# Remainders of the MLP operands by accumulating DMAs, in place of GpSimd and part of VectorE

## The chip, the cores and the metric

The kernel runs on one core of a Trainium2 chip, as one program. The metric is the device time of one execution in microseconds (us). Three runs of the kernel before gave a median of 1139.48 us (1139.41 to 1142.07). Five engines work in parallel, each through its own instruction stream: TensorE (PE; its weight loads are shown apart as PEld), VectorE (DVE), ScalarE (ACT), GpSimd (POOL) and SyncE (SP, which here only issues DMAs).

## The reference

One layer of a hybrid decoder (sequence 1024, width 1024, all in float32): a mixer (S5 state space and windowed attention) and a gated MLP. Only the MLP is touched by the change:

```python
h2 = _rms(x, norm2_w[l]) * (1 + sc2) + sh2
x = x + g2 * _conv_ffn(h2, w_up[l], conv_w[l], conv_b[l], w_down[l])

def _conv_ffn(h, w_up, conv_w, conv_b, w_down):
    up = h @ w_up                      # 1024x1024 by 1024x5632
    up = causal depthwise conv of width 3 (up) + conv_b
    val, gate = jnp.split(up, 2, axis=-1)
    return (jax.nn.silu(gate) * val) @ w_down      # 1024x2816 by 2816x1024
```

## The kernel before

**Precision.** A float32 operand is held as two halves: hi, its rounding to the format fp32r that TensorE multiplies, and lo, the remainder, again in fp32r. `split` (L137 to 141) makes them from a 128x512 operand: ScalarE copies the operand to hi with the rounding (L133 in the trace, a CAST), then VectorE or GpSimd subtracts, lo = operand - hi (L118, a TENSOR_TENSOR). Every product is three matmuls of 128x512 (`mm3`, L143 to 147; they stand at L97 or L99 in the trace): hi by hi, hi by lo, lo by hi.

**Two products by Strassen-Winograd.** Both MLP products work on 2x2 blocks with 7 block products instead of 8, numbered i = 1 to 7. Products 1, 2 and 4 take a block of the weights as it lies in DRAM (1 and 2 from the first row of blocks, 4 the last block); 3, 5, 6 and 7 take sums of blocks, which VectorE makes in place on the loaded tiles.

**The up product.** 22 f-tiles (FFT), for each of them 7 products of 12 matmuls. `weight(f, i)` (L949 to 970) makes the weight halves: `raw` loads two 128x1024 tiles of w_up by SP (at first tW, later tX4, tX5, W0, W1), and `split` writes into a ring of ten slots (tU0 to tU5 and four quarters of tXQ), seven products ahead. In it the lo of i = 1, 2, 4 is GpSimd's, the rest VectorE's. `took` (L1037 to 1058) copies or adds the PSUM banks, `conv` and a Silu follow, and `gd[f]`, the gated product in DRAM, is stored by SP (L1197).

**The lead part.** For f = 0 to 3 the products 1 and 2 run early, while VectorE and ScalarE still prepare the normalized operands A[3] to A[7]. The order of the matmuls is pinned there until f = 1, i = 5. Behind the first of these products stands `rms(1)`, on which the normalized operands of the second half of the sequence wait.

**The down product.** The 11 block rows p (256 columns of the gated product each) go in three chunks of 3, 4 and 4. In each chunk the products come in the order 1, 5, 6, 3, 7, 2, 4, and in each of these all p of the chunk: 77 steps of 12 matmuls. `fetch` loads the four blocks of gd and of w_down of one p; `operands` (L1130 to 1148) makes the sums, and for the two operands of a step `mixed` (L1121 to 1126) takes the next of nine slots and calls `split`, with every third lo on GpSimd ("vvp"). Operands are made three steps ahead (AH). `put` adds four banks to the output on VectorE (L127) after each product of a chunk. In steps 24 to 27 and 33 to 36 VectorE also adds the residual (xo + xt).

A scheduler arranges the instructions of each engine by the estimated time line; data dependences are kept.

Of the kernel before, what the change touches and what calls it, by code (L numbers as in the profile page):

```python
# [14 lines left out]
ADD, SUB, MUL, MAX, MIN = ALU.add, ALU.subtract, ALU.mult, ALU.max, ALU.min  # L15
# [7 lines left out]
FFT = 22  # L23
# [39 lines left out]
def hymba_kernel(ctx, tc, xT, c, wmod, wu, wkvq, small, consts, relb, pq, wglu, wout, wup, wdn, out):  # L63
# [7 lines left out]
    def new(tag, dt=F32):  # L71
        return pool.tile([128, SIZES.get(tag, 1024)], dt, tag=tag, name="t" + tag)
# [11 lines left out]
    def newr(tag):  # L84
        return RT(new(tag, F32R))

    vec, act, pol, sync = nc.vector, nc.scalar, nc.gpsimd, nc.sync
# [29 lines left out]
    def tt(eng, o, a, b, op):  # L117
        return eng.tensor_tensor(out=o, in0=a, in1=b, op=op)  # L118
# [12 lines left out]
    def cpy(e, o, i):  # L131
        if e == "a":
            act.copy(o, i)  # L133
        else:
            ENG[e].tensor_copy(out=o, in_=i)

    def split(x, src, hi_eng="a", lo_eng="v"):  # L137

        hi, lo = x
        cpy(hi_eng, hi.r, src)  # L140
        tt(ENG[lo_eng], lo.r, src, hi.f, SUB)

    def mm3(o, a, b, start, stop, chain=False):  # L143

        pe.matmul(o, a[0].r, b[0].r, start=start, stop=False, skip_group_check=chain)
        pe.matmul(o, a[0].r, b[1].r, start=False, stop=False, skip_group_check=chain)
        pe.matmul(o, a[1].r, b[0].r, start=False, stop=stop, skip_group_check=chain)
# [7 lines left out]
    def half(t):  # L155
        return t[:, 0:512], t[:, 512:1024]
# [82 lines left out]
    for k in range(8):  # L239
        xk = xs[k % 4]  # L240
        sync.dma_start(out=xk, in_=xT[k])
        emit_mod(8 + k, early[:, (k % 3) * 1024:(k % 3 + 1) * 1024], cact)
        if k % 2 == 0:
            wst = new(("W0", "A10")[k // 2 % 2])
            sync.dma_start(out=wst, in_=wu[k // 2])
        w = half(newr(f"U{k}") if k < 4 else wux[:, (k - 4) * 1024:(k - 3) * 1024])
        wus.append(w)
        split(w, wst[:, (k % 2) * 512:(k % 2) * 512 + 512])
        stt(mods[:, k:k + 1], mod[:, 8 + k:9 + k], 1.0, n1s[:, k:k + 1], ADD, MUL)
        hi, lo = hT[k]  # L250
        act.activation(out=hi.r, in_=xk, func=AF.Identity, scale=mods[:, k:k + 1])
        stt(lo.r, xk, mods[:, k:k + 1], hi.f, MUL, SUB)
        sq = new(("A11", "A1")[k % 2])
        act.activation(out=sq, in_=xk, func=AF.Square)
        if k == 0:
            sync.dma_start(out=cn, in_=consts[:, 0:384])
        for h in range(2):
            pe.matmul(bank[6 + h], ones, sq[:, h * 512:h * 512 + 512], start=(k == 0), stop=(k == 7))
        if k == 1:
            Q12, P12, Bs_t = new("W1"), new("U5"), new("U4")  # L260
            sync.dma_start(out=Q12, in_=pq[0])
            sync.dma_start(out=P12, in_=pq[1])
        for j in range(6):
            mm3(bank[j], sl(hT[k], slice(j, 1024, T)), w, k == 0, k == 7)
# [194 lines left out]
    def head_w(t):  # L459
        wst = new("W0")  # L460
        sync.dma_start(out=wst, in_=wkvq[t])
        w = (newr(f"U{2 * (t % 2)}"), newr(f"U{2 * (t % 2) + 1}"))
        split(w, wst)
        if t >= 2:
            qn.append(new(("W1", "U4", "U5")[t - 2]) if t < 5 else qx)
        b, b2, r = abank(), abank(), brow[:, (t % 2) * 128:(t % 2 + 1) * 128]
        for k in range(8):
            ks = slice(k * 128, k * 128 + 128)
            pe.matmul(b[0:2, 0:128], shs[:, 2 * k:2 * k + 2], w[0].r[:, ks], start=(k == 0), stop=False)
            pe.matmul(b[0:2, 0:128], shs[:, 2 * k:2 * k + 2], w[1].r[:, ks], start=False, stop=(k == 7))  # L470
        vec.tensor_copy(out=r, in_=b[0:2, 0:128])
        with pe.pin(False):
            pe.matmul(b2[:, 0:1], r, ones[0:2, 0:1], start=True, stop=True)
        vec.tensor_copy(out=bcol[:, t:t + 1], in_=b2[:, 0:1])
        return w
# [145 lines left out]
    for q in range(4):  # L621
        sync.dma_start(out=kd[:, 8 * q:8 * q + 8, 112:240],
                       in_=ka[32 * q:32 * q + 16, :].rearrange("p (g x) -> p g x", x=128))
# [60 lines left out]
    for h in range(2):  # L684
        for i in range(4):
            q_ = newr(f"H{8 + 4 * h + i}")
            for kv in range(2):
# [3 lines left out]
                src = qn[i][p0, h * 512:h * 512 + 512]  # L691
# [51 lines left out]
    for h in range(2):  # L743
        for m in range(4):
            zs[m, h] = half(newr(f"A{m + 4 * h}"))
            split(zs[m, h], zT[m][:, h * 512:h * 512 + 512], pick("ZH", m))
# [16 lines left out]
    for h in range(2):  # L763
# [9 lines left out]
        for n in range(4):  # L773
            src = zT[n][:, hs]
# [6 lines left out]
        for n in range(4):  # L781
            src = zT[n][:, hs]
# [27 lines left out]
    for n in range(8):  # L810
        av = bank[2]
        for kv in range(2):
            u = 2 * n + kv
            w_ = 256 if n else 128
# [4 lines left out]
            for i2 in range(2):  # L819
# [6 lines left out]
                for i1 in range(2):  # L826
                    i = 2 * i2 + i1
                    vec.tensor_tensor_reduce(  # L828
                        out=P[:, i, :], in0=b[:, i1 * 256:i1 * 256 + w_], in1=Tb[kv][:, i, 256 - w_:256],
# [31 lines left out]
    x = [xq[:, k * 1024:(k + 1) * 1024] for k in range(4)] + [new(f"X{k}") for k in range(4, 8)]  # L861
# [33 lines left out]
    for i, d in enumerate(order):  # L895
        if i % 2 == 0:
# [3 lines left out]
            w = (t_[:, 0:1024], t_[:, 1024:2048])  # L900
# [41 lines left out]
    def raw(f, which):  # L942
        i = ri[0]
        ri[0] += 1
        t_ = new(raws[i] if i < LEADS else (("X4", "W0"), ("X5", "W1"))[which][f % 2])
        sync.dma_start(out=t_, in_=wup[f + FFT * which])
        wraw[f, which] = half(t_)

    def weight(f, i):  # L949
        i_ = wi_[0]  # L950
        tag = ptags[i_ if i_ < 2 * LEADS else 2 + (i_ - 2 * LEADS) % 10]
        wi_[0] += 1
        if not isinstance(tag, str) and not wq:
            wq.append(newr("XQ"))
        w = half(newr(tag) if isinstance(tag, str) else wq[0][:, tag * 1024:(tag + 1) * 1024])
        wp[f, i] = w
        if (f, 0) not in wraw:
            raw(f, 0)
        v1, v2 = wraw[f, 0]
        if i not in (1, 2) and (f, 1) not in wraw:  # L960
            raw(f, 1)
        g1, g2 = wraw.get((f, 1), (None, None))
        if i == 5:
            tt(vec, v1, v1, g1, SUB)
            tt(vec, g1, g1, g2, ADD)
        elif i == 6:
            tt(vec, g1, g2, v1, SUB)
        elif i == 3:
            tt(vec, g1, v2, g1, SUB)
        split(w, {1: v1, 2: v2, 3: g1, 4: g2, 5: g1, 6: g1, 7: v1}[i], "a", "p" if i in (1, 2, 4) else "v")  # L970

    free = [5, 6, 7, 0, 1, 2, 3, 4]
    M = {}
# [9 lines left out]
    gd = [dp.tile([128, 1024], F32, name=f"gd{f}") for f in range(FFT)]  # L983
# [38 lines left out]
    A[1], A[2] = spots("S16"), spots("A9", "A10", "A11", "A12")  # L1022
    jobs = [lambda k=k: (normed(k, 0, rs), operand(1 + k // 4, k % 4, ht[k, 0])) for k in range(8)]
    jobs += [lambda f=f: (weight(f, 1), weight(f, 2)) for f in range(LEADS)]
    for d in range(lead, 12):
        if d == 4:
# [43 lines left out]
    for k in range(4):  # L1070
        normed(k, 1, rs)
        tt(vec, ht[k, 0], ht[k, 1], ht[k, 0], SUB)
        operand(5, k, ht[k, 0])
    weight(0, 5)
    for k in range(4):
        normed(k + 4, 1, rs)
        operand(3, k, ht[k + 4, 1])
        tt(vec, ht[k, 1], ht[k + 4, 1], ht[k, 1], SUB)
        tt(vec, ht[k + 4, 1], ht[k + 4, 1], ht[k, 0], SUB)
        operand(6, k, ht[k + 4, 1])  # L1080
    weight(0, 6)
    A[7] = spots("A4", "A5", "A6", "A7")
    for k in range(4):
# [12 lines left out]
    def conv(t_, tl, src):  # L1096
        act.activation(out=t_, in_=src, func=AF.Identity, scale=cw[:, 88 + tl:89 + tl], bias=S("conv_b", tl, 1))  # L1097
        for lag in (1, 2):
# [6 lines left out]
    homes = [("H4", "H5", "X4", "X5"), ("S16",), ("A9", "A10", "A11", "A12"), ("HA", "HB"),  # L1105
             ("H12", "H13", "H14", "H15"), ("A4", "A5", "A6", "A7"), ("A0", "A1", "A2", "A3"),
             ("H8", "H9", "H10", "H11"), ("S16",), ("A9", "A10", "A11", "A12"), ("H4", "H5", "X4", "X5")]
    cn_ = {"slot": 0, "split": 0}
    DEST = {1: (0, 0), 2: (0, 0), 3: (1, 0), 6: (1, 0), 5: (1, 1), 7: (1, 1), 4: (0, 1)}
    G, W = {}, {}  # L1110

# [6 lines left out]
                G[p, h, j] = ts_[j][:, h * 512:h * 512 + 512]  # L1118
                W[p, j, h] = ts_[2 + j][:, h * 512:h * 512 + 512]

    def mixed(v):  # L1121
        r_ = half(newr(SLOTS[cn_["slot"] % len(SLOTS)]))
        cn_["slot"] += 1
        split(r_, v, "a", "vvp"[cn_["split"] % 3])
        cn_["split"] += 1
        return r_

    SLOTS = ("U0", "U1", "U4", "U5", "U2", "U3", "A8", "H7", "H6")
# [1 line left out]
    def operands(i, p):  # L1130
        a11, a12, a21, a22 = W[p, 0, 0], W[p, 1, 0], W[p, 0, 1], W[p, 1, 1]
        b11, b12, b21, b22 = G[p, 0, 0], G[p, 1, 0], G[p, 0, 1], G[p, 1, 1]
        if i == 5:
            tt(vec, a11, a11, a21, SUB)
            tt(vec, a21, a21, a22, ADD)
            tt(vec, b11, b12, b11, SUB)
        elif i == 6:
            tt(vec, a21, a22, a11, SUB)
            tt(vec, b11, b22, b11, SUB)
        elif i == 3:  # L1140
            tt(vec, a21, a12, a21, SUB)
        elif i == 7:
            tt(vec, b12, b22, b12, SUB)
        elif i == 4:
            tt(vec, b11, b21, b11, SUB)
        w_ = {1: a11, 2: a12, 3: a21, 4: a22, 5: a21, 6: a21, 7: a11}[i]
        g_ = {1: b11, 2: b21, 3: b22, 4: b11, 5: b11, 6: b11, 7: b12}[i]
        return mixed(w_), mixed(g_)

    chunks = (range(0, 3), range(3, 7), range(7, 11))  # L1150
    steps = [(c_, i, p) for c_ in range(3) for i in (1, 5, 6, 3, 7, 2, 4) for p in chunks[c_]]
# [69 lines left out]
    for s_, (c_, i, p) in enumerate(steps):  # L1221
# [23 lines left out]
        elif p == ps_[-1]:  # L1245
            for d in range(4):
                for j, q_ in enumerate(ps_):
                    w_, g_ = ready[s_ - len(ps_) + 1 + j]
# [113 lines left out]
```

## Time and profile before

| | kernel before |
|---|---|
| median of three runs | 1139.48 us (1139.41 to 1142.07) |
| profiled execution, its own time | 1142.15 us |
| its span | 1140.3 us |
| mean granted TensorE clock | 0.958 |
| PE busy | 1053.4 us, 92% |
| DVE busy | 957.5 us, 84% |
| ACT busy | 550.2 us, 48% |
| POOL busy | 256.7 us, 23% |

The span is the profiler's, from the first to the last instruction; the time of an execution is some 2 us longer. Busy shares are means over stages of a different kind: the mixer up to about 450 us, the lead part to about 522 us, the up product to about 900 us and the down product to the end. All times within the trace are counted from the start of the span.

### The profile page before, as it was taken

How to read it: one execution, taken by the hardware profiler on the slowest of the kernel's cores; microseconds unless marked ns; L12 is line 12 of the kernel's file. 1: busy time of each engine (PE TensorE's matmuls, PEld its weight loads, DVE VectorE, ACT ScalarE, POOL GpSimd, SP SyncE). 2: the span in 40 equal slices, each digit the busy share in tenths (PEclk: the TensorE clock that was granted, in tenths of full speed). 3: DMA queues.
4: the chain of work that ended last, by engine and by line, in shares of the span. 5: the costliest groups of instructions: out<-in, count | busy, mean ns of one | idle time of the engine just before them, and what ended most of it. 6: DMA issues, size and time to landing. Idle time of an engine off the chain costs nothing.

```text
span 1140.3 us, 13281 instructions
## 1 busy us (share of the span) xinstructions
PE 1053.4 (92%) x4692; PEld 828.2 (73%) x4692; DVE 957.5 (84%) x1541; ACT 550.2 (48%) x936; POOL 256.7 (23%) x137
## 2 busy tenths in 40 slices
PE   6979999688989899779999999999999989989998
PEld 4868777475646577657888888888888768768876
DVE  8996899969988988888777878797777787997985
ACT  5412443583874346745554545455444554434342
POOL 0000000002121001762122223212212142353541
PEclk9979999679989899989999999999999989999999
DMA  9501516025024743222223232423123359120002
GB/s 371 214 19 39 127 40 93 1 88 190 19 94 183 240 147 112 93 92 93 93 78 113 87 130 93 151 90 112 56 93 126 115 217 384 63 93 1 1 37 111
DMA packets 47333, 128.13 MB, mean 112 GB/s; under 512 B 6017, under 2 KB 13985, under 8 KB 47266
## 3 DMA queue, kind: packets, MB, share of 16 engines
q1 hardware_dynamic: 47266, 127.28, 32.8%
q8 instruction: 37, 0.61, 0.2%
q14 instruction: 30, 0.25, 0.1%
HBM read 105.28 MB, written 21.99 MB: 112 GB/s over the span
## 4 chain that ended last, share of the span: by engine, by line
PE 60%; DVE 29%; ACT 4%; DMA 3%; issue 3%; POOL 1%; SPq 0%; ACTq 0%; DVEq 0%; POOLq 0%
PE bk L97 54%; PE bk L99 6%; DVE tA L118 5%; DVE tU L118 3%; DVE tH L118 3%; DVE tS L118 2%; DVE tX L127 2%; DMA tW<-in_dram 2%; DVE bk L118 2%; DVE tS L180 1%; DVE tXQ L118 1%; DVE tXQ L127 1%; DVE tX L118 1%; DVE tX L180 1%; ACT tU L133 1%
## 5 line engine op out<-in xcount | busy, mean ns | idle before, releaser
L97 PE MATMUL bk<-tU,tU 128*128 128x512 f32 x516 | 124.9, 395 | 4.8 <-DVE tXQ L127 2.4
L97 PE MATMUL bk<-tA,tU 128*128 128x512 f32 x516 | 128.1, 395 | 0.8 <-DVE tA L118 0.8
L97 PEld LDWEIGHTS bk<-tU,tU 128*128 128x128 f32 x516 | 97.6, 190 | 27.8 <-issue 2.8
L97 PE MATMUL bk<-tH,tU 128*128 128x512 f32 x477 | 116.0, 392 | 0.0
L97 PEld LDWEIGHTS bk<-tA,tU 128*128 128x128 f32 x516 | 96.7, 188 | 24.2 <-DVE tA L118 1.4
L127 DVE SCALAR_TENSOR_TENSOR tX<-tH,sm,tX 128x1023 f32<-128x1023 f32 x66 | 100.5, 1523 | 8.0 <-ACT tX L1097 7.9
L97 PEld LDWEIGHTS bk<-tH,tU 128*128 128x128 f32 x477 | 89.1, 188 | 19.3
L97 PE MATMUL bk<-tA,tXQ 128*128 128x512 f32 x300 | 76.0, 401 | 2.1 <-ACT tH L1050 2.1
L118 POOL TENSOR_TENSOR tU<-tW,tU 128x512 fp32r<-128x512 f32 x25 | 36.3, 1462 | 174.1 <-ACT tU L133 152.4
L97 PE MATMUL bk<-tH,tA 128*128 128x512 f32 (+1 forms) x168 | 63.9, 509 | 11.4 <-ACT tH L133 7.6
L133 ACT CAST tU<-tW 128x512 fp32r<-128x512 f32 (+1 forms) x67 | 47.1, 710 | 48.9 <-PE bk L97 18.2
L97 PEld LDWEIGHTS bk<-tA,tXQ 128*128 128x128 f32 x300 | 57.4, 191 | 16.0 <-ACT tH L1050 2.5
L99 PE MATMUL bk<-tH,tU 128*128 128x512 f32 x267 | 64.0, 395 | 1.8 <-DVE tU L118 1.7
L118 POOL TENSOR_TENSOR tH<-tH,att 128x1024 f32<-128x1024 f32 (+1 forms) x9 | 19.1, 2124 | 195.8 <-DVE att L840 161.7
L118 DVE TENSOR_TENSOR tX<-tX,tX 128x512 f32<-128x512 f32 (+1 forms) x63 | 61.6, 981 | 0.8
L118 POOL TENSOR_TENSOR tXQ<-tW,tXQ 128x512 fp32r<-128x512 f32 x12 | 49.1, 4102 | 53.1 <-ACT tXQ L133 37.8
L99 PEld LDWEIGHTS bk<-tH,tU 128*128 128x128 f32 x267 | 49.6, 189 | 15.6 <-DVE tU L118 2.7
L97 PE MATMUL bk<-tXQ,tH 128*128 128x256 f32 (+2 forms) x224 | 51.9, 374 | 4.3 <-DVE att L828 4.3
L118 DVE TENSOR_TENSOR tU<-tW,tU 128x512 fp32r<-128x512 f32 (+2 forms) x43 | 37.8, 881 | 20.4 <-ACT tU L133 20.4
L97 PEld LDWEIGHTS bk<-tXQ,tH 128*128 128x128 f32 x224 | 45.1, 268 | 13.3 <-DVE att L828 9.0
L118 POOL TENSOR_TENSOR tU<-tX,tU 128x512 fp32r<-128x512 f32 x19 | 33.2, 1747 | 84.9 <-ACT tU L133 70.8
L118 DVE TENSOR_TENSOR tU<-tX,tU 128x512 fp32r<-128x512 f32 x39 | 31.3, 808 | 23.6 <-ACT tU L133 23.6
(349 smaller groups left out, 2398.9 us busy)
## 6 DMA issues: line engine op xcount, KB each, us to landing
tX<-in_dram SPq DMA_DIRECT2D x51, 512.0 KB, 3.3
tW<-in_dram SPq DMA_DIRECT2D x49, 512.0 KB, 3.3
tS<-in_dram SPq DMA_DIRECT2D x30, 512.0 KB, 6.0
gd<-tX SPq DMA_DIRECT2D x22, 512.0 KB, 2.9
tA<-in_dram SPq DMA_DIRECT2D x12, 512.0 KB, 9.7
tH<-in_dram SPq DMA_DIRECT2D x12, 512.0 KB, 4.2
tH<-gd SPq DMA_DIRECT2D x8, 512.0 KB, 4.7
tA<-gd SPq DMA_DIRECT2D x8, 512.0 KB, 8.9
```

Source lines behind the costliest of these rows:

```text
L97: return f(*a, **k)
L99: i = f(*a, **k)
L118: return eng.tensor_tensor(out=o, in0=a, in1=b, op=op)
L127: return vec.scalar_tensor_tensor(out=o, in0=a, scalar=s, in1=b, op0=op0, op1=op1)
L133: act.copy(o, i)
L180: vec.tensor_tensor_reduce(out=st, in0=st, in1=ca, scale=1.0, scalar=S("b_mod", j, 1), op0=MUL, op1=ADD, accum_out=mod[:, j:j + 1],)
```

## The change

A new way to make the two halves, `asplit`, is used where the operand also lies unchanged in DRAM. ScalarE copies it to hi as before, ScalarE writes the negative of hi to lo, and a DMA issued by GpSimd reads the 128x512 block (256 KB) from DRAM again and adds it onto lo. It is used for the weights of i = 1, 2, 4 in the up product (66 splits), and in the down product for the weights of i = 1, 2, 4 and the gated product of i = 1, 2, 3 (66 splits). All other splits have their lo on VectorE; the pattern "vvp" is gone. GpSimd has no subtraction left in the MLP.

```diff
+    def asplit(x, src, dram):
+        hi, lo = x
+        act.copy(hi.r, src)
+        act.mul(lo.r, hi.f, -1.0)
+        pol.dma_start(out=lo.r, in_=dram, accum_op=ADD)
...
     def weight(f, i):
...
-        split(w, {1: v1, 2: v2, 3: g1, 4: g2, 5: g1, 6: g1, 7: v1}[i], "a", "p" if i in (1, 2, 4) else "v")
+        if i in (1, 2, 4):
+            asplit(w, {1: v1, 2: v2, 4: g2}[i], wup[f + (FFT if i == 4 else 0)][:, 0 if i == 1 else 512:512 if i == 1 else 1024])
+        else:
+            split(w, {3: g1, 5: g1, 6: g1, 7: v1}[i])
...
-    def mixed(v):
+    def mixed(v, dram=None):
...
-        split(r_, v, "a", "vvp"[cn_["split"] % 3])
-        cn_["split"] += 1
+        if dram is None:
+            split(r_, v)
+        else:
+            asplit(r_, v, dram)
...
-        return mixed(w_), mixed(g_)
+        lo, hi = slice(0, 512), slice(512, 1024)
+        wd = {1: wdn[2 * p][:, lo], 2: wdn[2 * p + 1][:, lo], 4: wdn[2 * p + 1][:, hi]}.get(i)
+        gp = {1: gd[2 * p][:, lo], 2: gd[2 * p + 1][:, lo], 3: gd[2 * p + 1][:, hi]}.get(i)
+        return mixed(w_, wd), mixed(g_, gp)
```

In the changed kernel the copy of `asplit` stands at L146, the multiplication at L147 and the DMA at L148; later lines move down by 7 to 15.

Lead part, ScalarE, before: the copies of the weights of f = 0 (from tW0) and f = 1 (from tW1), and between them a square for `rms(1)` (L999) and the copy of the first bank (L1040).

```order
L133 CAST tU2_3284<-tW0_3285 128x512
L133 CAST tU3_3289<-tW0_3285 128x512
L999 ACTIVATE tA7_3123<-tX7_2637 128x512
L133 CAST tU2_3324<-tW1_3325 128x512
L1040 COPY tA8_3353<-bk5_68 128x512
```

The same place in the changed kernel (the square is now L1009, the copy of the bank L1050):

```order
L146 CAST tU2_3284<-tW0_3285 128x512
L146 CAST tU3_3290<-tW0_3285 128x512
L147 ACTIVATE tU2_3284<-tU2_3284 128x512
L147 ACTIVATE tU3_3290<-tU3_3290 128x512
L1009 ACTIVATE tA7_3123<-tX7_2637 128x512
L146 CAST tU4_3320<-tW0_3321 128x512
L146 CAST tU5_3326<-tW0_3321 128x512
L147 ACTIVATE tU4_3320<-tU4_3320 128x512
L147 ACTIVATE tU5_3326<-tU5_3326 128x512
L146 CAST tU2_3330<-tW1_3331 128x512
L1050 COPY tA8_3361<-bk5_68 128x512
```

ScalarE now makes both copies before the first negation, and the square and the bank's copy come behind more work.

Down product, GpSimd, before: subtractions of every third operand, from sums (tHB, tA) as from blocks as loaded.

```order
L118 TENSOR_TENSOR tH6_6981<-tA6_6613,tH6_6981 128x512
L118 TENSOR_TENSOR tU4_7004<-tA0_6696,tU4_7004 128x512
L118 TENSOR_TENSOR tU3_7051<-tH14_6525,tU3_7051 128x512
L118 TENSOR_TENSOR tH6_7073<-tA5_6612,tH6_7073 128x512
L118 TENSOR_TENSOR tU4_7118<-tHB_6456,tU4_7118 128x512
```

GpSimd in the changed kernel, at the products 3 and 2 of the second chunk (four p each; in_12_dram is w_down, gd the gated product):

```order
L148 DMA tU2_7123<-gd7_2881 128x512
L148 DMA tA8_7147<-gd9_2883 128x512
L148 DMA tH6_7167<-gd11_2885 128x512
L148 DMA tU1_7196<-gd13_2887 128x512
L148 DMA tU1_7295<-in_12_dram 128x512
L148 DMA tU4_7299<-gd7_2881 128x512
L148 DMA tU5_7319<-in_12_dram 128x512
L148 DMA tU2_7323<-gd9_2883 128x512
```

Its stream holds only DMA issues there: one for each step of product 3, two for each step of product 2.

TensorE at the step where product 1 of the last chunk begins, before, one step of 12 matmuls (weights from tU0, gated product from tH6):

```order
L97 MATMUL bk1_64<-tU0_7366,tH6_7363 128x512 x3
L97 MATMUL bk2_65<-tU0_7366,tH6_7363 128x512 x3
L97 MATMUL bk0_63<-tU0_7366,tH6_7363 128x512 x3
L97 MATMUL bk3_66<-tU0_7366,tH6_7363 128x512 x3
```

The same step in the changed kernel:

```order
L97 MATMUL bk1_64<-tU0_7475,tH6_7471 128x512
L97 MATMUL bk2_65<-tU0_7475,tH6_7471 128x512
L97 MATMUL bk0_63<-tU0_7475,tH6_7471 128x512
L97 MATMUL bk1_64<-tU0_7475,tH6_7471 128x512 x2
L97 MATMUL bk2_65<-tU0_7475,tH6_7471 128x512 x2
L97 MATMUL bk0_63<-tU0_7475,tH6_7471 128x512 x2
L97 MATMUL bk3_66<-tU0_7475,tH6_7471 128x512 x3
```

Three matmuls that need only the two hi halves now come first, and those with a lo half behind them.

## Rows read from the trace of the kernel before

**Rows 1.** The page: busy time by engine; the chain that ended last, by engine.
```profile
PE 1053.4 (92%) x4692; PEld 828.2 (73%) x4692; DVE 957.5 (84%) x1541; ACT 550.2 (48%) x936; POOL 256.7 (23%) x137
PE 60%; DVE 29%; ACT 4%; DMA 3%; issue 3%; POOL 1%; SPq 0%; ACTq 0%; DVEq 0%; POOLq 0%
```

**Rows 2.** Windows (from:to, length, then busy us and instructions by engine).
```profile
core 0: us, PE busy (x) PEld busy (x) DVE busy (x) ACT busy (x) POOL busy (x), PEclk, DMA share, GB/s
475.00:500.00 25.00, 12.21 (x38) 8.36 (x37) 25.00 (x43) 13.04 (x24) 25.00 (x1) 0.73 0.12 40
700.00:800.00 100.00, 100.00 (x435) 81.50 (x434) 82.98 (x93) 53.91 (x78) 25.17 (x16) 1.00 0.30 107
895.00:925.00 30.00, 23.25 (x87) 17.85 (x86) 29.66 (x36) 16.73 (x25) 9.08 (x4) 0.84 0.05 20
925.00:961.00 36.00, 36.00 (x158) 29.50 (x157) 26.77 (x32) 19.29 (x35) 13.26 (x10) 0.99 1.00 392
1000.00:1040.00 40.00, 35.00 (x140) 26.70 (x139) 36.82 (x47) 14.88 (x27) 18.56 (x10) 0.96 0.19 66
1040.00:1090.00 50.00, 50.00 (x219) 40.67 (x218) 46.42 (x65) 19.35 (x34) 24.55 (x12) 1.00 0.00 1
```

**Rows 3.** Chain that ended last, in order of time (start us, us, what).
```profile
453.18 1.29 POOL tU L118
454.51 2.61 PE bk L99 x10
...
459.73 4.27 POOL tU L118 x3
...
499.88 1.11 DVE tXQ L118
500.99 1.71 DVE tU L118
...
521.90 371.67 PE bk L97 x1604
...
1136.60 0.75 DVE tX L127
```

**Rows 4.** Time line of single instructions (start us, us, engine, line, operation).
```profile
451.96 0.63 ACT L999 ACTIVATE tA<-tX 128x512 f32<-128x512 f32 x1 [0.49 <-DVE tX L127]
452.50 1.12 ACT L133 CAST tU<-tW 128x512 fp32r<-128x512 f32 x2
455.73 0.33 SPq L946 DMA_DIRECT2D tW<-in_dram  x1
469.29 31.15 POOL L118 TENSOR_TENSOR tXQ<-tW,tXQ 128x512 fp32r<-128x512 f32 x1 [5.30 <-ACT tXQ L133]
907.58 2.31 DVE L127 SCALAR_TENSOR_TENSOR tX<-tH,sm,tX 128x1023 f32<-128x1023 f32 x1
912.21 1.27 DVE L127 SCALAR_TENSOR_TENSOR tX<-tH,sm,tX 128x1022 f32<-128x1022 f32 x1
927.03 0.69 DVE L118 TENSOR_TENSOR tH<-tH,tH 128x512 f32<-128x512 f32 x1
927.64 1.78 DVE L118 TENSOR_TENSOR tH<-tA,tH 128x512 fp32r<-128x512 f32 x1
929.12 1.45 POOL L118 TENSOR_TENSOR tH<-tA,tH 128x512 fp32r<-128x512 f32 x1 [0.24 <-ACT tH L133]
```

**Rows 5.** Groups by form from 895 us on (line, engine, out<-in, count | busy us, mean ns).
```profile
L118 POOL TENSOR_TENSOR tU<-tA,tU 128x512 fp32r<-128x512 f32 x12 | 22.8, 1901 | 43.2 <-ACT tU L133 43.2
...
L127 DVE SCALAR_TENSOR_TENSOR tXQ<-bk,mod,tXQ 128x512 f32<-128x512 f32 x40 | 27.9, 740 | 7.4 <-PE bk L97 7.4
```

**Rows 6.** The page, DMA issues: out<-in, count, KB each, median us from issue to landing.
```profile
tX<-in_dram SPq DMA_DIRECT2D x51, 512.0 KB, 3.3
...
gd<-tX SPq DMA_DIRECT2D x22, 512.0 KB, 2.9
...
tA<-in_dram SPq DMA_DIRECT2D x12, 512.0 KB, 9.7
```

More of the change, by code (lines that the diff above doesn't have):

```diff
@@ L1107, in hymba_kernel @@
              ("H8", "H9", "H10", "H11"), ("S16",), ("A9", "A10", "A11", "A12"), ("H4", "H5", "X4", "X5")]
-    cn_ = {"slot": 0, "split": 0}
+    cn_ = {"slot": 0}
     DEST = {1: (0, 0), 2: (0, 0), 3: (1, 0), 6: (1, 0), 5: (1, 1), 7: (1, 1), 4: (0, 1)}
```

## The prediction

> **What bounds the kernel now.** I read the page's totals and its chain first, then a table of windows over the MLP, and last the chain and single instructions where a window shows TensorE short of work.
>
> TensorE is busy for 92% of the span and DVE for 84%; the chain is 60% PE and 29% DVE, and POOL has 1% of it [rows 1]. So GpSimd's own work is hardly ever what ends last. What matters is whom its work slows, and where.
>
> By stage: from 521.90 to 893.57 the chain is one piece of 1604 matmuls, 371.67/1604 = 0.2317 us each [rows 3], and the window 700 to 800 agrees (PE 100.00 of 100, clock 1.00) [rows 2]. This is the up product. DVE is at 83%, ACT at 54%, POOL at 25%: none of them holds PE up.
>
> Two windows of the down product lose time. From 895 to 925 PE did 87 matmuls, worth 20.2 us at 0.2317: 9.8 us lost, the clock at 0.84, DVE busy for 29.66 of 30 us. From 1000 to 1040 it did 140, worth 32.4: 7.6 lost, DVE at 36.82 of 40. The windows 925 to 961 and 1040 to 1090 lose nothing, the latter though DVE is busy for 46.42 of 50 us [rows 2]. So some 17.4 us can be won in the down product, and both places are DVE's.
>
> The lead part loses more (475 to 500: PE 12.21 of 25, clock 0.73, DVE 25.00 of 25) [rows 2], but the DVE work there, normalized operands, is not touched by the change.
>
> Why DVE is late: GpSimd's subtraction and DVE's two-input operations hold each other up. A DVE subtraction takes 0.69 us and starts 0.61 us behind the one before it; the next, beside a POOL subtraction of 1.45 us, takes 1.78. The convolution's step takes 1.27 us, and 2.31 beside POOL. The other way, one POOL subtraction that began at 469.29, when DVE ran without a gap, took 31.15 us [rows 4]. Each POOL operation in a busy DVE stretch therefore costs DVE 1.04 to 1.09 us. "SBUF — State Buffer" of the Trainium skill (section "🔬 SBUF: two separate sides") states this as an exclusive lock on a shared port pair, held for the whole instruction against a DVE operation with two SBUF inputs. The trace agrees, with 1.78 against 0.69 us.
>
> **The change part by part.**
>
> It removes 66 GpSimd subtractions in the up product and 51 in the down product, and 15 net of DVE's (103 to 88 in the down product). It adds 132 negations on ACT, and 132 DMAs of 256 KB from GpSimd, 34.6 MB.
>
> *Up product, 0 us.* Each f-tile is 84 matmuls, 19.5 us, and gets three ACT operations of 0.63 us [rows 4], 1.9 us: ACT goes from 54% to about 64%. Three DMAs per tile add 0.79 MB, some 40 GB/s. TensorE covers all this as long as the lo halves land in time. By the changed order the slot of an i = 1 weight is free 33 to 41 matmuls before its lo is wanted (7.6 to 9.5 us), that of i = 2 longer (10.6 to 19). Of it 0.62 us goes to the copy, 0.63 to the negation, 0.1 to the hand-overs: 6.3 us at the least are left for issue and landing of the DMA.
>
> *The price of such a DMA.* No accumulating DMA, and none from GpSimd, is in the trace of before. The nearest rows are SP's: 0.33 us to issue [rows 4], and 3.3 us to land for 512 KB in the median, 2.9 for the store of gd, 9.7 where the loads collide [rows 6]. Half the bytes could halve 2.9: lower end 1.5, upper end 9.7 + 0.33 = 10.0. I take 3.3 + 0.33 = 3.6 us, half the bytes against the read and write-back of the destination. Then nothing stalls. The page "DMA: Bandwidth & Descriptors" of the Trainium skill (section "🔬 Anatomy of one DMA — SWDGE (gpsimd) path") fits a transfer issued by GpSimd with 2.0 us plus its bytes divided by 436,000 per us; by that an estimate for 256 KB is 2.6 us, and the sum would be the same. No row here shows such a transfer.
>
> *Lead part, +1.5 us.* Before, two copies end at 453.62 [rows 4], POOL's lo of tU2 at 454.47, and PE starts its ten waiting matmuls at 454.51 [rows 3]. In the changed order the first negation comes behind both copies: 453.62 + 0.55 = 454.2, then 3.6 for the DMA: 457.8, 3.3 us later, and rms(1) is queued behind it (bounds: 1.5 gives 455.7, +1.2; 10.0 gives 464.2, +9.7). Against that, POOL's three subtractions of 4.27 us at 459.73 are gone, and so is what POOL did to DVE at 499.88 and 500.99: 1.11 and 1.71 us [rows 3] for operations of 0.61, 1.6 us. Together +3.3 - 1.6 = 1.7, of which I take 1.5; bounds -1 and +8.
>
> *895 to 925, -5 us.* DVE's list in this stretch sheds the lo's of product 1 (four of six, at 0.61: 2.4 us) and the delays by four POOL operations [rows 2] (4 x 1.05 = 4.2); it takes on the third that POOL had of product 5 (two, 1.2). Net 5.4 us of a chain that is DVE's end to end. Bounds 0 and -9.8.
>
> *1000 to 1040, -6 us.* Take products 1, 5, 6, 3 of the second chunk, 16 steps, 16 x 12 x 0.2317 = 44.5 us of PE. DVE before: for each of four p 0 + 3 + 2 + 1 sums and 4 x 1.33 lo's, 45.3 x 0.61 = 27.6; 10.7 POOL operations at 1.05 (they took 1.90 in the mean [rows 5]) = 11.2; four times four bank additions of 0.74 [rows 5] = 11.8; eight residual additions of twice the width, 8 x 1.2 = 9.8 at twice 0.61: 60.4 us, 16 too many, of which running ahead hides half. After: sums 6 and lo's 0 + 2 + 2 + 1 per p, 44 x 0.61 = 26.8, with 11.8 and 9.8: 48.4 us, 3.9 too many, which the run-ahead covers but for one or two. Product 1 now asks nothing of DVE, and since the lo no longer reads the loaded tile, the sums of product 5 can be made in that time. Bounds 0 and -7.6.
>
> *Products 1, 2 and 4 of the down part, 0 us.* ACT has four operations a step, 2 x 0.62 + 2 x 0.63 = 2.5 us in 2.78 (0.52 apart when back to back [rows 4]). DVE is nearly idle there. With nine slots, the gated product's slot is free three steps before it is wanted, 8.3 us, the weight's four steps, 11.1; 8.3 - 1.35 leaves 6.9 for the DMA. From 925 to 961 the DMA share is already 1.00 at 392 GB/s [rows 2]; the last loads of this burst may land later, but PE had 36.00 of 36 there. Bounds 0 and +33 (below).
>
> Sum: +1.5 - 5 - 6 = -9.5 us. The profiled execution had 1142.15 us on a span of 1140.3; it would become 1132.6 on 1130.8. It lies 2.7 above the median of the runs, so the median becomes 1139.5 - 9.5 = 1130.
>
> **The rivals.**
>
> *A: the accumulating DMA lands too late (slower).* Place: the lo of i = 1 in each up tile, and products 1, 2, 3 of the down part. It decides from issue + landing = 6.3 us. At 8.0 the way from free slot to lo is 9.35 us: against 8.55 (the middle of 7.6 and 9.5) 0.8 us are lost in 18 tiles, 14 us; in the down product three steps have to last 9.35, 3.12 each instead of 2.78, 0.34 x 33 = 11; the lead part pays 454.2 + 8.0 - 454.5 - 1.6 = 6; less the 11 won: 1139.5 + 20 = 1160. At 10.0 the way is 11.35: 2.8 x 18 = 50, 1.0 x 33 = 33, 8, less 11: 1220. For it: the 9.7 of [rows 6], the read and write-back that no row shows. Against: half the bytes, and a DMA share near 0.30 in the up product [rows 2].
>
> *B: GpSimd issues late beside a busy DVE (slower).* If issuing needs what the 31.15 us subtraction waited for [rows 4], the DMAs wait for gaps of DVE. In products 1 and 2 DVE is idle; in the up product it has gaps (17%); the price is paid at product 3, where residual additions run beside it: some 1 us in 11 steps, and with half of it in 18 tiles, 20 us less the 11: about 1148. In the Trainium skill, "SBUF — State Buffer" (section "🔬 SBUF: two separate sides", the box on DVE blocking a DMA) says that GpSimd can't write descriptors while DVE holds the pair, 620 ns becoming 3100; it says so for copies in a two-port mode. No row shows such a DMA.
>
> *C: no difference.* DVE now has five operations a step in product 5 (3.05 us against 2.78) and four in product 6, all lo's its own; or ACT's copies wait behind negations. Then what POOL's absence gives is lost to the crowding, and the lead part's 1.5 remain less a little: 1139. For it: the DVE count falls by 15 of 1541 only. Against: 1040 to 1090, where DVE at 93% costs PE nothing [rows 2].
>
> **How the numbers follow.** Forecast 0.54, A 0.22, B 0.08, C 0.16. A measurement of this kernel can tell 0.3% (3.4 us) from no change. Faster: the forecast and a little of C, 0.56; same: most of C and some of B, 0.16; slower: A and the rest, 0.28. The forecast's own range is 1139.5 - 17.4 = 1122 to 1136. The range goes up to A at 8.0 us, 1160, and leaves A's worse half out.
>
> **What would show it.** Right: the two losing windows of the down product with PE busy for over 27 of 30 and over 38 of 40 us, DVE two-input operations at 0.6 to 0.7 us throughout, POOL without long rows, the lo DMAs landing in 3 to 4 us, the first big piece of PE beginning 1 to 2 us later. Wrong: PE waiting for a DMA of tU or tXQ in the up product (A); POOL issues far behind their negations (B); PE waits in products 5 and 6 as long as before (C). The forecast falls if the landing is above 6 us.

## The result, and the profile after

The changed kernel took 1149.41 us in the median of four runs (1147.94 to 1149.63), the kernel before 1140.31 us on the same chip. The ratio is 1.0075, with a 95% interval of 1.0058 to 1.0093: slower by 9 us, where 9.5 us less were forecast. The profiled execution took 1147.94 us on a span of 1146.2.

The page of the changed kernel, busy time by engine and the DMA queues (packets, MB, share of 16 engines' span):

```profile
PE 1054.6 (92%) x4692; PEld 829.9 (72%) x4692; DVE 881.1 (77%) x1526; ACT 618.9 (54%) x1068; POOL 145.2 (13%) x152
...
q1 hardware_dynamic: 47266, 127.28, 32.9%
q0 software_dynamic: 19008, 34.61, 18.7%
```

DVE and POOL shed what they were to shed (957.5 and 256.7 us before [rows 1]), and the time grew all the same. The new queue carries 34.61 MB, about a quarter of the old one's 127.28, but holds the DMA engines more than half as long: 1.85 MB per point of share against 3.87.

The windows of the changed kernel:

```profile
core 0: us, PE busy (x) PEld busy (x) DVE busy (x) ACT busy (x) POOL busy (x), PEclk, DMA share, GB/s
...
475.00:500.00 25.00, 14.05 (x50) 10.24 (x48) 25.00 (x43) 15.05 (x28) 0.86 (x1) 0.80 0.21 49
...
700.00:800.00 100.00, 100.00 (x435) 81.35 (x435) 68.12 (x86) 56.77 (x87) 12.95 (x15) 1.00 0.57 147
...
895.00:925.00 30.00, 27.69 (x115) 22.24 (x114) 29.56 (x41) 21.79 (x34) 4.31 (x5) 0.94 0.43 96
925.00:961.00 36.00, 31.77 (x128) 25.25 (x127) 15.95 (x25) 23.26 (x43) 9.57 (x11) 0.91 1.06 326
961.00:1000.00 39.00, 31.30 (x119) 24.60 (x118) 25.64 (x40) 17.31 (x31) 7.88 (x9) 0.86 0.96 292
1000.00:1040.00 40.00, 39.13 (x171) 31.83 (x170) 33.86 (x51) 21.38 (x38) 7.36 (x9) 1.00 0.46 107
1040.00:1090.00 50.00, 49.77 (x217) 40.39 (x216) 41.53 (x67) 28.70 (x52) 13.57 (x16) 1.00 0.60 94
```

Against [rows 2]: the two windows that lost time have become fuller, 115 matmuls for 87 and 171 for 140. The one from 925 to 961, which was full with a DMA share of 1.00, has 128 for 158, and the next has 119 matmuls where the kernel before had 165:

```profile
961.00:1000.00 39.00, 37.66 (x165) 30.47 (x164) 38.90 (x52) 16.39 (x30) 13.81 (x8) 1.00 0.33 122
```

In both windows of the changed kernel the DMA share is about 1. In the first it was full before too, but now fewer bytes move in it (326 GB/s for 392); in the second it was 0.33.

What TensorE waited for from 440 us on in the changed kernel (engine, line, waited for: us in total, times, longest):

```profile
PE bk L99 <- DVE tU L118: 8.0, 2, 5.7
PE bk L97 <- DMA tU<-gd: 7.1, 3, 3.9
PE bk L99 <- DMA tU<-in_dram: 6.2, 1, 6.2
PE bk L97 <- DVE tA L118: 5.7, 1, 5.7
...
PE bk L97 <- DMA tH<-gd: 2.0, 1, 2.0
```

The three waits for a DMA are new, and the wait for DVE at tA was 0.8 us before. A tU or tH that TensorE takes from a DMA is an accumulating lo, since TensorE reads only halves. The 5.7 us for DVE at line 118 (tA) are a wait for a DMA at second hand: the time line of DVE in the changed kernel shows it standing before a residual addition whose xd had not landed,

```profile
978.64 1.23 DVE L118 TENSOR_TENSOR tXQ<-tXQ,tH 128x1024 f32<-128x1024 f32 x1 [8.98 <-DMA tH<-xd]
```

and its chain names the loads that came last:

```profile
452.30 5.58 DMA tU<-in_dram
...
947.70 8.17 DMA tU<-gd
...
960.84 17.71 DMA tH<-xd
```

The plain load of xd, issued by SP, took 17.71 us. The four such loads between 925 and 998 took 16.3 us in the median, against 5.1 in the kernel before; the DMA views of that stretch (40 slices of the DMA share, then these loads), before and after:

```profile
DMA  9999999999999999996989999810800000000000
...
tH<-xd SPq DMA_DIRECT2D x4, 512.0 KB, 5.1
```

```profile
DMA  9999999999999999999999999999999999999980
...
tH<-xd SPq DMA_DIRECT2D x4, 512.0 KB, 16.3
```

Before, the loads were through some 50 us after 925; with the accumulating transfers beside them the engines are full for all 73 us.

To see where the time went I set the starts of the 4692 matmuls of two traces side by side. The profiled execution of before was 2.7 us above its median, and up to 422.9 us, in work that no kernel here changes, it lags behind every other by 0.2 to 3.4 us; so each row below counts from there. The columns are the time in the trace of before; the entries, us gained (-) or lost (+) since the matmul at 422.9.

Each row is one execution. Lead on VectorE and both have the same lead part, and so have the two kernels with the lead on GpSimd; in the column 533 each pair differs by 1.7 us. Differences below 2 us between two rows are therefore not read as an effect.

| kernel | 533 (up product begins) | 879 | 930 | 953 | 988 | 1032 | end |
|---|---|---|---|---|---|---|---|
| changed | +3.5 | +3.7 | -2.7 | -2.0 | +16.4 | +7.6 | +7.5 |
| up only | +3.6 | +3.8 | +1.4 | +1.4 | +1.4 | +1.4 | +1.6 |
| down only | -0.3 | -0.4 | -1.5 | -0.9 | +13.8 | +5.3 | +4.6 |
| all on VectorE | +3.4 | +3.4 | -2.3 | -2.3 | -2.4 | -3.6 | -4.8 |
| plain DMAs | +2.7 | +2.9 | -4.4 | -3.2 | +3.0 | -6.3 | -7.6 |
| no burst | +4.1 | +4.3 | -3.0 | -3.0 | -3.1 | -5.9 | -1.6 |
| lead on VectorE | +1.7 | +1.9 | -5.3 | -3.0 | +13.1 | +3.8 | +4.2 |
| both | +3.4 | +3.6 | -2.3 | -2.3 | -2.3 | -5.5 | -4.3 |
| up on VectorE, no burst | +3.2 | +3.2 | +0.2 | +0.2 | +0.1 | -3.7 | -2.3 |
| lead on GpSimd, no burst | -0.5 | +0.5 | -5.5 | -5.5 | -5.6 | -9.1 | -8.3 |
| lead on GpSimd, no DMA | +1.2 | +1.2 | -4.1 | -4.1 | -4.1 | -6.2 | -7.4 |

The first row is the result in one line: +3.5 in the lead part, nothing in the up product, -6.4 at the start of the down product, +18.5 between 953 and 988, -8.8 behind it.

Not all of the 18.5 us is waiting. TensorE waits three times there, 3.88, 2.03 and 5.67 us, together 11.6. Behind such a wait its granted clock is lower: from 955.9 to 959.7 it is 0.50 (the level of 1.2 GHz), and 8 matmuls take 3.78 us, twice the 0.2317 us each of the up product:

```profile
955.91 3.78 PE L97 MATMUL bk<-tU,tU 128*128 128x512 f32 x8 [3.88 <-DMA tU<-gd]
```

The remaining 7 us of the stall are such slower matmuls.

### The profile page after: what moved, and what is told of

Its sections match the earlier page's. It is cut to its first block, busy times and chain, and to the rows that moved or that the text cites. A ratio compares the mean times of both kernels' runs of the same rounds, so it can differ in the third digit from the quotient of the medians.

```text
span 1146.2 us, 13550 instructions
## 1 busy us (share of the span) xinstructions
PE 1054.6 (92%) x4692; PEld 829.9 (72%) x4692; DVE 881.1 (77%) x1526; ACT 618.9 (54%) x1068; POOL 145.2 (13%) x152
## 3 DMA queue, kind: packets, MB, share of 16 engines
q1 hardware_dynamic: 47266, 127.28, 32.9%
q0 software_dynamic: 19008, 34.61, 18.7%
## 4 chain that ended last, share of the span: by engine, by line
PE 60%; DVE 22%; DMA 8%; issue 4%; ACT 4%; POOL 0%; SPq 0%; DVEq 0%; POOLq 0%; ACTq 0%
PE bk L97 53%; PE bk L99 8%; DVE tA L118 3%; DVE tS L118 2%; DVE tH L118 2%; DVE tU L118 2%; DVE bk L118 2%; DMA tU<-gd 2%; DMA tH<-xd 2%; DVE tX L127 1%; DMA tW<-in_dram 1%; DVE tS L187 1%; DMA tU<-in_dram 1%; DVE tX L187 1%; DMA tH<-gd 1%
## 5 line engine op out<-in xcount | busy, mean ns | idle before, releaser
L97 PE MATMUL bk<-tA,tU 128*128 128x512 f32 x516 | 132.5, 402 | 5.7 <-DVE tA L118 5.7
L97 PEld LDWEIGHTS bk<-tA,tU 128*128 128x128 f32 x516 | 99.1, 192 | 29.6 <-DVE tA L118 6.1
L148 POOL DMA_DIRECT2D tU<-in_dram x66 | 61.9, 952 | 364.4 <-ACT tU L147 211.5
L127 DVE SCALAR_TENSOR_TENSOR tX<-tH,sm,tX 128x1023 f32<-128x1023 f32 x66 | 84.4, 1279 | 6.4 <-ACT tX L1107 6.1
L118 DVE TENSOR_TENSOR tX<-tX,tX 128x512 f32<-128x512 f32 (+1 forms) x63 | 55.4, 889 | 0.9 <-DMA tX<-in_dram 0.5
L147 ACT ACTIVATE tU<-tU 128x512 fp32r<-128x512 f32 x87 | 53.2, 626 | 1.1
L97 PEld LDWEIGHTS bk<-tXQ,tH 128*128 128x128 f32 x224 | 43.9, 263 | 13.1 <-DVE att L835 9.3
L118 DVE TENSOR_TENSOR tU<-tX,tU 128x512 fp32r<-128x512 f32 x36 | 24.6, 687 | 30.4 <-ACT tU L133 30.3
L97 PE MATMUL bk<-tH,tXQ 128*128 128x512 f32 x192 | 47.0, 391 | 0.0
L97 PEld LDWEIGHTS bk<-tH,tA 128*128 128x128 f32 (+1 forms) x168 | 26.9, 173 | 25.0 <-issue 7.6
L133 ACT CAST tU<-tW 128x512 fp32r<-128x512 f32 (+1 forms) x42 | 31.8, 762 | 23.9 <-DMA tW<-in_dram 13.8
```

The costliest lines, as they stand in the source:

```text
L97: return f(*a, **k)
L127: return vec.scalar_tensor_tensor(out=o, in0=a, scalar=s, in1=b, op0=op0, op1=op1)
L147: act.mul(lo.r, hi.f, -1.0)
L148: pol.dma_start(out=lo.r, in_=dram, accum_op=ADD)
```

## The experiments

Theory: the DMA engines are full while the loads of the second chunk run (925 to 998), and an accumulating DMA takes about twice a plain one's share of them; there the lo's and the loads come late. Rivals: GpSimd issues late beside a busy DVE; the three-step window is too short for this DMA anywhere; the loss is the lead part's.

**Up product only.** The down product splits as before (every third lo on GpSimd).

```diff
-        if dram is None:
-            split(r_, v)
+        cn_["split"] += 1
+        if True:
+            split(r_, v, "a", "vvp"[(cn_["split"] - 1) % 3])
```

> Only the up product's 66 splits use the accumulating DMA; the down product is as before. Theory (the DMA engines are full when the down product's loads meet accumulating DMAs, and the lead part waits for the first lo): about +3.5 us from the lead part, nothing in the down product, 1143 to 1145 us. Rival (the issues of GpSimd come late beside a busy DVE, wherever they are): the same lead loss and stalls at the i = 1 weights of the up product, over 1146.

Measured: 1144.67 us (1141.63 to 1145.84) against 1139.58, ratio 1.004 (1.0027 to 1.0054). The loss is in the lead part, +3.6, as expected, and 42% of DMA engine time lies unused in the up product (700 to 800). TensorE waited for a weight's DMA once, 6.0 us at the first weight of the lead part, and behind it for none.

**Down product only.**

```diff
         if i in (1, 2, 4):
+            split(w, {1: v1, 2: v2, 4: g2}[i], "a", "p")
+        elif False:
             asplit(w,
```

> Only the down product's 66 splits use the accumulating DMA and its other lo's VectorE; the up product is as before. Theory: the gains at the start of the down product (5 us) and at 1000 to 1040 stand, the stall between 925 and 1000 stands too (16 us): 1142 to 1146 us, with the DMA share near 1.0 from 925 to beyond 990. Rival (the loss is the lead part's, the down product wins as predicted): 1130 to 1134.

Measured: 1147.08 us (1144.87 to 1149.24), ratio 1.007 (1.0052 to 1.0088), a little over the expected. The stall between 953 and 988 is there, 14.7 us, with the lead part undisturbed. That the loss is the lead part's falls. But the gain at the start of the down product is 1.1 us where I expected 5: TensorE waits there for two accumulating lo's, 3.5 us for one of gd and 1.0 for one of w_down.

**Every lo on VectorE.** No accumulating DMA, no GpSimd subtraction.

```diff
         if i in (1, 2, 4):
+            split(w, {1: v1, 2: v2, 4: g2}[i])
+        elif False:
             asplit(w,
...
-        if dram is None:
+        if True:
             split(r_, v)
```

> No accumulating DMA and no GpSimd subtraction: every lo of both MLP products on VectorE. Theory (VectorE's delay by GpSimd is worth more than the subtractions): VectorE gets 117 subtractions more than before but none is held up; the up product stays at TensorE's rate, the down product wins 3 to 6 us: 1134 to 1138 us. Rival (what VectorE sheds is the work, not the waiting): 117 x 0.61 us more on a late VectorE, 1143 to 1150.

Measured: 1135.61 us (1132.43 to 1138.31), ratio 0.9964 (0.9953 to 0.9976). VectorE has 117 instructions more than before and the same busy time, 957.4 us for 957.5 [rows 1]:

```profile
PE 1052.0 (93%) x4692; PEld 829.5 (73%) x4692; DVE 957.4 (84%) x1658; ACT 549.3 (48%) x936; POOL 30.5 (3%) x20
```

In busy time GpSimd's subtractions had thus cost VectorE as much as doing them itself. To take GpSimd out is a gain by itself; the DMAs turned it into a loss.

**Plain DMAs.** The 132 DMAs overwrite lo instead of adding, so the remainders aren't computed.

```diff
-        pol.dma_start(out=lo.r, in_=dram, accum_op=ADD)
+        pol.dma_start(out=lo.r, in_=dram)
```

> As the changed kernel, but the 132 DMAs overwrite lo with the operand instead of adding (the remainder is then not computed; same bytes read, same instructions). Theory (an accumulating DMA occupies the DMA engines for about twice its bytes, and these are full between 925 and 1000): the software queue's share falls by half, the stall of 16 us falls to 5 to 9, the lead loss shrinks by 1: 1138 to 1144 us. Rival (lateness of the issue or of the negation): as the changed kernel, 1148 to 1150.

Measured: 1132.86 us (1132.35 to 1135.10), ratio 0.9945 (0.9931 to 0.9959), against 1.0075 for the changed kernel, and better than I expected. The same 34.61 MB now hold 10.7% of the engines' span; the row of its page, and then its DMA view from 925 to 998 (queue; then out<-in, count, KB, median us to landing):

```profile
q0 software_dynamic: 19008, 34.61, 10.7%
```

```profile
q1 hardware_dynamic: 4894, 17.82, 63.5%
q0 software_dynamic: 2880, 5.24, 21.9%
...
tU<-in_dram POOLq DMA_DIRECT2D x7, 256.0 KB, 8.7
```

The same view of the changed kernel:

```profile
DMA  9999999999999999999999999999999999999980
...
q1 hardware_dynamic: 4914, 17.86, 63.9%
q0 software_dynamic: 2880, 5.24, 39.2%
...
tU<-in_dram POOLq DMA_DIRECT2D x7, 256.0 KB, 12.5
```

In 73 us the loads need 63.9%, 46.6 us of all engines. The 20 accumulating DMAs add 39.2%, 28.6 us, 1.43 us each: together 103%, and the engines are full to the end. Plain ones add 21.9%, 16.0 us, 0.80 each: 85%, and the stall between 953 and 988 is 6.2 us instead of 18.5. Both kernels read the same 34.6 MB, so two thirds of the stall come with the accumulation. (The values that TensorE multiplies differ too; nothing here tests whether that matters for the time.) Its issue costs GpSimd more too, by the groups of the two kernels from 522 us on (changed first):

```profile
L148 POOL DMA_DIRECT2D tXQ<-in_dram x23 | 19.9, 863 | 121.0 <-ACT tXQ L147 73.6 <-PE bk L97 14.9 <-DVE tA L118 14.0
```

```profile
L148 POOL DMA_DIRECT2D tXQ<-in_dram x23 | 12.1, 528 | 127.8 <-ACT tXQ L147 78.7 <-PE bk L97 15.6 <-DVE tA L118 14.6
```

**No accumulating DMA in the burst.** Of the down product's 66, the 20 of products 3, 2, 4 of the first chunk and of product 1 of the second become VectorE's subtractions.

```diff
+        if p < 3 and i != 1 or p in chunks[1] and i == 1:
+            wd = gp = None
         return mixed(w_, wd), mixed(g_, gp)
```

> As the changed kernel, but with VectorE's subtraction in place of the accumulating DMA for the products 3, 2 and 4 of the first chunk and product 1 of the second, the steps whose DMAs fall into the loads of 925 to 1000 (16 of 132 DMAs less... 3 + 6 + 3 + 8 = 20). Theory (the loss is DMA engines full in this stretch): the stall of 18 us goes but for 1 to 3 us, and the 7 us given back behind it are given back no more; the lead loss stays: 1134 to 1139 us. Rival (the window of three steps is too short for an accumulating DMA anywhere in the down product): at most the 20 removed DMAs' share, 1145 to 1148.

Measured: 1139.37 us (1135.23 to 1142.34), ratio 0.9996 (0.9984 to 1.0009), at the edge of what I expected. The stall is gone to the last microsecond (-3.0 at 953, -3.1 at 988), as its windows show:

```profile
925.00:961.00 36.00, 36.00 (x159) 29.57 (x158) 28.24 (x46) 20.70 (x37) 0.00 (x0) 1.00 1.02 412
961.00:1000.00 39.00, 37.97 (x165) 30.55 (x165) 39.00 (x61) 19.14 (x33) 1.73 (x2) 1.00 0.31 108
```

The loads still fill the engines in the first window, as in [rows 2], but nothing waits for them. The rival of a window too short anywhere allowed 1 to 4 us; by the two ratios (1.0075 and 0.9996) 9 us came. It is not gone altogether: outside the burst TensorE still waits for lo's by DMA, 7.4 us in all, and all of it behind 895:

```profile
PE bk L97 <- DMA tU<-gd: 4.4, 2, 2.3
PE bk L97 <- DMA tU<-in_dram: 2.3, 1, 2.3
PE bk L97 <- DMA tH<-gd: 0.7, 1, 0.7
```

Two of these waits, 2.3 and 0.7 us, lie behind 1032, where this kernel gives 4.3 us back.

**Lead part on VectorE.** The weights of f = 0 to 3 (products 1, 2 and also 4: twelve) are split by VectorE.

```diff
-        if i in (1, 2, 4):
+        if i in (1, 2, 4) and f >= LEADS:
```

> As the changed kernel, but the eight weights of the lead part (f = 0 to 3) have their lo on VectorE. Theory (the lead loss of 3.5 us is the first lo's landing): 1145 to 1147 us, and no wait of TensorE for a DMA of tU near 455. Rival (VectorE is the bound there, eight subtractions more cost it what the DMA did): 1148 to 1150.

Measured: 1147.23 us (1142.86 to 1148.15), ratio 1.006 (1.0046 to 1.0074). The expected time, but the intervals of this and of the changed kernel overlap, so this pair alone doesn't tell. Its profiled execution, 1142.86 us, was the fastest of its six, 4.4 us below their median.

**Both edits.**

> Both edits: VectorE's lo's in the lead part and in the 20 places of the load burst, accumulating DMAs elsewhere (104). Theory: the two losses add up and are gone: 1130 to 1135 us. Rival: as in the two runs beside it, 1143 to 1148.

Measured: 1135.22 us (1134.07 to 1137.67), ratio 0.9963 (0.9951 to 0.9975), at the upper edge of the expected, 4.2 us below the run with the burst's edit alone. In the traces 1.5 us of that lies before 422.9, where the two kernels are the same; at 1032 the table has this one no better (-5.5 for -5.9), and 2.7 us come behind. (100 accumulating DMAs remain; the 104 in the expectation left product 4 out of the lead weights.) TensorE no longer waits for a DMA at the first lo, and yet the up product begins 3.4 us late: its waits from 440 to 525 are

```profile
PE bk L99 <- ACT tU L133: 7.9, 2, 7.4
PE bk L99 <- DVE tU L118: 7.9, 3, 4.1
PE bk L97 <- ACT tH L1060: 2.1, 1, 2.1
```

**The up product on VectorE, no DMA in the burst.**

```diff
-        if i in (1, 2, 4):
+        if False:
```

> The whole up product's lo's on VectorE, and the accumulating DMA only in the down product outside the load burst (46 DMAs). Theory (the up product is at TensorE's rate either way): as the run before it, within 2 us, 1130 to 1135. Rival (VectorE's load in the up product matters to the clock or to the hand-over at its end): over 1136, as with every lo on VectorE.

Measured: 1137.18 us (1133.07 to 1138.10), ratio 0.9971 (0.996 to 0.9982), beyond the expected 1135 and in the rival's range; the interval overlaps that of the run before it. The trace shows 3.0 us gained at the hand-over to the down product, between 879 and 930, where that one has 5.9. But VectorE's load in the up product, the rival's reason, doesn't explain this: the kernel with every lo on VectorE has the same up product and gains 5.7 there. What differs is that TensorE waits here for two accumulating lo's, 4.0 us for one of gd and 1.2 for one of w_down, against 2.5 for one of gd in the run before it. Why they land later here is open.

**Lead part on GpSimd.** As with both edits, but the eight weights of products 1 and 2 of f = 0 to 3 have their lo on GpSimd, as before the change.

```diff
+        if i in (1, 2, 4) and f < LEADS and i < 3:
+            split(w, {1: v1, 2: v2}[i], "a", "p")
+        elif i in (1, 2, 4) and f >= LEADS:
```

> As the kernel with both edits, but the eight weights of products 1 and 2 of f = 0 to 3 have their lo on GpSimd, as in the kernel before (100 accumulating DMAs remain, none in the lead part and none in the load burst). Theory (in the lead part VectorE is the bound, and GpSimd's subtraction, which takes 1.3 us there, was the cheap place; the DMA's landing and VectorE's extra subtractions each lose the same 3.4 us): 3 us less, 1131 to 1133 us. Rival (the lead loss is the scheduler's other order, or GpSimd delays VectorE there as much): 1134 to 1136.

Measured: 1132.45 us (1132.17 to 1134.11), ratio 0.9947 (0.9935 to 0.996): the lowest time of the kernels that compute the whole result, 0.5% below the kernel before and, by the two ratios, 1.3% below the changed one. In its trace the lead loss is gone (-0.5 at 533). The times alone don't show that: the interval overlaps that of both edits.

**Lead part on GpSimd, no accumulating DMA.**

> No accumulating DMA at all: GpSimd has the lo of the eight lead weights, VectorE all others. Theory as beside it: 3 us less than with every lo on VectorE, 1131 to 1134 us, so that the accumulating DMAs outside the burst are worth 0 to 2 us. Rival (the DMAs are needed to relieve VectorE in the later products of the down part): 1135 or more.

Measured: 1133.70 us (1132.73 to 1134.75), ratio 0.9955 (0.9941 to 0.9968), in the expected range, though by the two ratios it is 1.0 us and not 3 below every lo on VectorE, with intervals that overlap. Its interval and that of the run before it overlap as well: the 100 accumulating DMAs of the kernel beside it are worth no more than can be measured, though they take 100 subtractions off VectorE.

## Why the prediction was wrong

**The step that failed: "Products 1, 2 and 4 of the down part, 0 us".** It said that the last loads of the burst may land later, "but PE had 36.00 of 36 there". That row showed a resource with nothing left: a DMA share of 1.00 [rows 2]. TensorE was full there, so the operands came early enough; by how much, the row does not say. I reckoned the price of one DMA as its latency against the window of one slot, not its share of full engines, and so missed that it also holds up the plain loads behind it. The runs: +18.5 us between 953 and 988; 6.2 with plain DMAs; 0 without the 20 in the burst. Of the 18.5, 5.9 us were waits for lo's that landed late, 5.7 came through DVE's 8.98 us before xd, and the rest was slower matmuls at the lower clock behind these waits.

The step failed at a second place too, away from the burst. At the third step of product 1 in the first chunk, with a DMA share of 0.52 (905 to 915), TensorE waited 2.3 us for a lo of gd in the changed kernel, and 2.3 to 4.0 us in every run with accumulating DMAs there; with plain ones it was 0.8.

Two of the signs of being right came true all the same: PE was busy for 27.69 of 30 us and 39.13 of 40 in the two windows. The gains were looked for where the change should win, and the loss came where the sum had a zero.

**The price of the DMA was too low.** I took 3.6 us for issue and landing. In the up product it was 0.86 and 4.1 to 4.5; the view from 700 to 800 in the changed kernel:

```profile
tU<-in_dram POOLq DMA_DIRECT2D x9, 256.0 KB, 4.1
...
tXQ<-in_dram POOLq DMA_DIRECT2D x6, 256.0 KB, 4.5
```

That is some 5.4 us, under the 6.3 from which rival A was to decide, and the up product did lose nothing: that step held. In the burst it landed after 7 to 12.5 us, above the 6.9 of the down product's window. So rival A's mechanism is what happened, at one of its places and for another reason than it gave: its 1160 was built on the up product's 18 tiles and all 33 steps.

**Lead part, +1.5: it was +3.5.** The first lo came at 457.87 (bounds 455.7 and 464.2; 457.8 forecast), and TensorE waited 6.2 us there. That the time agrees is luck: this trace was 2.2 us ahead when the two copies began (450.33 for 452.50 [rows 4]), and the DMA took 5.58 us where I had put 3.6. From the start of the copies to the ten waiting matmuls it is 7.6 us for 2.0 before, 5.6 more, not 3.3:

```profile
450.33 1.14 ACT L146 CAST tU<-tW 128x512 fp32r<-128x512 f32 x2
457.92 4.63 PE L99 MATMUL bk<-tS,tU 128*128 128x512 f32 x10 [6.18 <-DMA tU<-in_dram]
```

But the price at 533 is not that landing alone. With VectorE in its place the wait is 1.5 us (both edits), and the loss is still 3.2 to 3.4 us in three traces and 1.7 in a fourth; with GpSimd in its place it is -0.5 and +1.2. What the two dear ways share is that the work of the lead weights moves from an idle GpSimd to a path on which DVE and ACT are late; which of their queued instructions pays I can't name, and it stays open.

**895 to 925, -5: it was -6.4.** The convolution step at that place shows one of the terms, 1.28 us for 2.31 [rows 4]:

```profile
907.37 1.28 DVE L127 SCALAR_TENSOR_TENSOR tX<-tH,sm,tX 128x1023 f32<-128x1023 f32 x1
```

But the size is partly luck. My list of what DVE sheds holds only work of the down product, and the down product's change alone gave 1.1, with 4.5 us of waits for accumulating lo's against it; the up product's alone gave 2.4. The forecast had no term for either.

One reading in the forecast was off, without consequence: the subtraction beside DVE's 1.78 us row was not the one of 929.12, which began as that row ended, but the one before it:

```profile
927.25 1.62 POOL L118 TENSOR_TENSOR tU<-tS,tU 128x512 fp32r<-128x512 f32 x1 [1.46 <-ACT tU L133]
```

**1000 to 1040, -6: it was -8.8,** but behind a stall in which DVE's sums could run ahead. Without the stall the same stretch gives 2.8 to 3.8 in the four kernels that have accumulating DMAs in the down product but none in the burst (product 1 of the second chunk is VectorE's in them), and 1.2 to 2.1 in the two without any. So the term was too large, by about half.

**Rival B did not happen.** From 475 to 500 DVE was busy without a gap in both kernels. Before, the POOL subtraction there took 31.15 us [rows 4]; after, the issue in the same stretch took 0.86:

```profile
483.02 0.86 POOL L148 DMA_DIRECT2D tU<-in_dram  x1 [8.79 <-ACT tU L147]
```

The DVE operations in that stretch of the changed kernel are all TENSOR_TENSOR. "SBUF — State Buffer" of the Trainium skill (section "🔬 SBUF: two separate sides") describes the stall of descriptors written by GpSimd for DVE operations in a two-port mode, and says that tensor_tensor did not show it. The trace agrees: the issue took 0.86 us, the mean of those from 522 us on (863 ns). So rival B's condition, that issuing needs what the subtraction waited for, did not hold beside these operations.

## What to carry to other kernels

Before moving work onto DMAs, look for windows where the DMA share is already 1: there a transfer is priced by its share of the engines, and the plain loads behind it pay too. In this kernel an accumulating DMA counted 1.8 times a plain one in that sum. And when two engines hold each other up, first try the plain cure: VectorE alone did all 117 subtractions in the busy time that it had needed beside GpSimd.

## What the runs showed of the hardware

An accumulating DMA of 256 KB in float32 from DRAM onto SBUF held all 16 engines for 1.43 us in the burst, a plain one issued by GpSimd 0.80; over the span, 18.7% against 10.7% for 132 of them, 1.62 us each against 0.92. It took GpSimd 0.86 us to issue, against 0.53, and it took 4.1 to 4.5 us to land between 700 and 800, against 3.1 to 3.4. The four plain loads of xd (512 KB each, by SP) took 16.3 us in the median beside 20 of them, against 5.1 in the kernel before. Behind a wait of 3.9 us TensorE's granted clock was 0.50, and a matmul of 128x512 took 0.47 us instead of 0.23.
